# Mixer gates: all side projections first, the last four gate pairs by seven block products

## The chip, the cores and the metric

One core of one Trainium2 chip runs the whole program in one launch. The time is device microseconds of one execution; the number given for a kernel is the median of its runs.

## The reference

Three layers follow each other on 512 rows (528 with 16 meta rows in the first two) of width 1024: a layer with differential attention, one with latent attention, and a block that mixes a convolution and a sliding-window attention. Each ends in a gated feed-forward with a convolution of width 3. All is fp32. The change lies in the mixer of the last block:

```
u = rmsnorm(x, norm_mix_w)
proj = u @ w_in + b_in
cb, cc, cx, q, k, v, g_conv, g_attn = split(proj)
y_conv = (cb * causal_dwconv(cc * cx, conv_mix_w)) @ w_conv_out
y_attn = sliding_window_attention(rope(q), rope(k), v, sinks) @ w_attn_out + b_attn_out
merged = sigmoid(g_conv) * y_conv + sigmoid(g_attn) * y_attn
x = x + merged @ w_mix_out
```

## The kernel before

Activations are held transposed: 128 channels on the partitions, the 512 rows along the free dimension, eight such tiles for the width of 1024. Each fp32 operand is held as two fp32r parts, hi and lo, and a product is three matmuls per 128 channels of contraction: hi hi, hi lo, lo hi (`lin`, L331 to 345).

Weights come through `Weights`. A plan lists the chunks in the order of use; `get` hands out the next chunk and, with it, splits the two that follow and loads the three that follow. A load goes by SP's queue into one of three `raw` buffers. A split is a cast on ACT to `whi` (L176) and a subtraction to `wlo`, on DVE in two halves of 512 columns (L184), or, for one chunk in four, on POOL in pieces of 256 columns (L114).

The feed-forwards compute some of their products in another way, which the change brings to the gates. Two weight tiles (a and b of one f) against two halves of the rows and two halves of the contraction make a two by two block product; `Seven` gets it with seven block products of 12 matmuls each instead of eight, and adds the results together in PSUM and with u1 and u2. Its inputs T are differences of the activations, made once per feed-forward. Its weights are of four kinds: "a" is a chunk as loaded (with its partner in a second buffer, `rawA`), and "s", "t", "d" come from four sums that POOL makes of the two loads (`combine`: 512 columns each, in halves of 256, L114). "s" and "d" have a single buffer each.

The mixer (L1651) first makes Y, the convolution's result, and OT, the attention's, both as hi and lo. Then, in the stage around the change, it goes over eight tiles t. For each it computes two gates (`pg`, 24 matmuls each, X against a chunk of `w_in2`), multiplies them by the norm R on DVE (L1821), takes the sigmoid on ACT (L1822); then the two sides, `pyc` from Y (24 matmuls) and `pya` from OT (12), which DVE takes out of PSUM while it multiplies by the gates (L1826, L1829). POOL adds the two (L1830, below called the join) and the sum is split to MG on ACT and DVE (L450, L451). After that `proj_h` multiplies MG by `w_mo` (`po`) and adds into h.

A scheduler sets the order of the instructions on every engine when the program is built; where code runs inside `in_order`, PE keeps the order in which it is written. Each engine then runs its instructions in that order, and a waiting instruction holds all behind it on its engine.

Of the kernel before, what the change touches and what calls it, by code (L numbers as in the profile page):

```python
# [21 lines left out]
P = 128  # L22
D = 1024
KD = D // P
META = 16
SEQ = 512
NT = META + SEQ
# [15 lines left out]
def _layout_params():  # L43
# [38 lines left out]
class Weights:  # L82
# [126 lines left out]
class Pair:  # L209
# [5 lines left out]
    def at(self, k, s, e):  # L215
        c = slice(s - self.t0, e - self.t0)
        return self.hi[:, k, c], self.lo[:, k, c]


class Net:  # L220
    def __init__(self, ctx, tc, ins, out):
        self.tc, self.nc, self.I, self.out = tc, tc.nc, ins, out
# [1383 lines left out]
    def tables2(self):  # L1606
# [40 lines left out]
            nc.vector.tensor_copy(bandb, band)  # L1647
        self.tables = C, S, bandb


    def mixer(self):  # L1651
        nc, tc = self.nc, self.tc
        scale = 64 ** -0.5
        with ExitStack() as cx:
            e = cx.enter_context
            X, xcx = self.X, self.xcx
            xp = e(tc.tile_pool(name="m2x", bufs=1, side="right", reuse_waits="tile"))
            tp = xcx.enter_context(tc.tile_pool(name="m2t", bufs=2, reuse_waits="tile"))
            acx = ExitStack()
            psm = acx.enter_context(tc.tile_pool(name="m2pm", bufs=2, space=PSUM, reuse_waits="tile"))  # L1660
            pss = acx.enter_context(tc.tile_pool(name="m2ps", bufs=1, space=PSUM, reuse_waits="tile"))
# [3 lines left out]
            R = self.norm2(pss, "s")[:, META:]  # L1665
# [7 lines left out]
            Y = self.xpair(xp, "Y2", KD, META)  # L1673
# [27 lines left out]
            C, S, bandb = self.tables  # L1701
            at = acx.enter_context(tc.tile_pool(name="m2at", bufs=2, reuse_waits="tile"))
# [38 lines left out]
            t = pst.tile([P, 512], F32, tag="t", name=self.n("vt"))  # L1741
# [5 lines left out]
            OT = self.xpair(xp, "OT2", 4, META)  # L1747
# [62 lines left out]
            MG = self.xpair(e(tc.tile_pool(name="m2g", bufs=1, side="right", reuse_waits="tile")), "MG", KD, META)  # L1810
            for t in range(8):
                wgc = [(self.W.get(("w_in2", 30 + t, 0)), 0)]
                wga = [(self.W.get(("w_in2", 38 + t, 0)), 0)]
                wco = [(self.W.get(("w_co", t, 0)), 0)]
                wao = [(self.W.get(("w_ao", t, 0)), 0)]
                g = []
                for w, b, tag in ((wgc, 30 + t, "y"), (wga, 38 + t, "pr")):
                    ps = psm.tile([P, 512], F32, tag="mm", name=self.n("pg"))
                    self.lin(ps, w, X, META, NT)
                    z = tp.tile([P, SEQ], F32, tag=tag, name=self.n("sg"), bufs=2)  # L1820
                    nc.vector.tensor_tensor(z, ps, R, op=ALU.mult)  # L1821
                    nc.scalar.activation(z, z, AF.Sigmoid, bias=self.pc("b_in", b))  # L1822
                    g.append(z)
                ps = psm.tile([P, 512], F32, tag="mm", name=self.n("pyc"))
                self.lin(ps, wco, Y, META, NT)
                nc.vector.tensor_tensor(g[0], ps, g[0], op=ALU.mult)  # L1826
                ps = psm.tile([P, 512], F32, tag="mm", name=self.n("pya"))
                self.lin(ps, wao, OT, META, NT)
                nc.vector.scalar_tensor_tensor(g[1], ps, self.pc("b_ao", t), g[1], op0=ALU.add, op1=ALU.mult)  # L1829
                nc.gpsimd.tensor_tensor(g[0], g[0], g[1], op=ALU.add)  # L1830
                self.split(*MG.at(t, META, NT), g[0])
            xcx.close()
            self.open_x("ffn2_norm", META)
            self.proj_h(psm, "w_mo", MG, REAL)

# [127 lines left out]
```

## Time and profile before

| | us |
|---|---|
| median of 3 runs | 2060.43 (2058.05 to 2063.83) |
| the profiled execution | 2064.14 |
| its span | 2062.4 |
| PE, DVE, ACT, POOL busy | 2036.0, 1400.2, 980.5, 719.1 |

The profile is of one execution. PE's busy time is modelled, so full busy does not mean full speed; how long a group of matmuls takes is read from the chain of waits. In rows of groups the mean of one instruction is in ns. Records of neighbours on one engine can overlap by some hundredths of a us.

### The profile page before, as it was taken

The page shows a single profiled execution, that of the slowest core. Times are in us where ns is not written, and L with a number is a line of the kernel's source. Part 1 is how long each engine was busy: PE and PEld are TensorE (multiplying, and loading weights), DVE is VectorE, ACT ScalarE, POOL GpSimd, SP SyncE. Part 2 cuts the span into 40 slices and gives each one's busy share as a digit, 9 for nine tenths or more (in the row PEclk, how much of TensorE's full clock was granted, in tenths as well). Part 3 has the DMA queues.
Part 4 walks back from the last instruction along what each step waited for, and adds up shares of the span by engine and source line. Part 5 has one row for each costly group of instructions (what it writes and reads, how often), then busy time and mean ns, then how long its engine had stood idle before and what let it go on. Part 6 is the DMA issues. An engine that isn't in the chain of part 4 may idle for free.

```text
span 2062.4 us, 36284 instructions
## 1 busy us (share of the span) xinstructions
PE 2036.0 (99%) x14314; PEld 1884.8 (91%) x14314; DVE 1400.2 (68%) x2548; ACT 980.5 (48%) x1967; POOL 719.1 (35%) x818
## 2 busy tenths in 40 slices
PE   8999999999999999999999999999999999999998
PEld 8999899999999989899899898888888889999897
DVE  8788768667677576668667687675433358667684
ACT  6666545434355455455435355454332335445353
POOL 5222252435353331132536355321022242436452
PEclk9999999999999999999999999999999999999999
DMA  5121132333323111032332322222223232322322
GB/s 172 53 62 52 42 105 68 106 93 98 99 84 98 53 41 42 32 99 74 100 102 92 110 85 89 87 92 72 67 81 104 97 113 70 105 93 99 116 72 72
DMA packets 56426, 174.91 MB, mean 85 GB/s; under 512 B 6464, under 2 KB 9408, under 8 KB 56256
## 3 DMA queue, kind: packets, MB, share of 16 engines
q1 hardware_dynamic: 55824, 172.34, 26.4%
q8 instruction: 112, 1.84, 0.4%
q14 instruction: 58, 0.48, 0.1%
q10 hardware_dynamic: 432, 0.27, 0.0%
HBM read 170.45 MB, written 2.10 MB: 84 GB/s over the span
## 4 chain that ended last, share of the span: by engine, by line
PE 87%; DVE 8%; ACT 2%; issue 1%; POOL 1%; DMA 0%; ACTq 0%; DVEq 0%; SPq 0%
PE po L343 24%; PE pf L576 18%; PE pf L343 17%; PE pc L343 6%; PE pg L343 4%; PE pyc L343 2%; PE pq L343 2%; PE s L767 2%; DVE wlo L184 2%; PE ph L343 2%; PE pm L343 2%; PE pd L343 1%; PE o L1422 1%; PE pya L343 1%; DVE nm L777 1%
## 5 line engine op out<-in xcount | busy, mean ns | idle before, releaser
L176 ACT CAST whi<-raw 128x512 fp32r<-128x512 f32 (+4 forms) x484 | 384.7, 808 | 532.9 <-PE po L343 154.5
L114 POOL TENSOR_TENSOR wlo<-raw,whi 128x256 fp32r<-128x256 f32 (+1 forms) x316 | 273.9, 894 | 572.7 <-ACT whi L176 537.3
L184 DVE TENSOR_TENSOR wlo<-raw,whi 128x512 fp32r<-128x512 f32 (+2 forms) x590 | 410.7, 731 | 50.6 <-ACT whi L176 47.3
L343 PE MATMUL pf<-Xl,whi 128*128 128x256 f32 (+2 forms) x960 | 271.2, 283 | 0.9 <-DVE Xl L454 0.9
L343 PE MATMUL pf<-Xh,whi 128*128 128x256 f32 (+2 forms) x960 | 271.4, 283 | 0.0
L343 PE MATMUL pf<-Xh,wlo 128*128 128x256 f32 (+2 forms) x960 | 271.4, 283 | 0.0
L343 PE MATMUL po<-Gh,wlo 128*128 128x512 f32 (+2 forms) x710 | 239.4, 338 | 0.0
L343 PE MATMUL po<-Gl,whi 128*128 128x512 f32 (+2 forms) x710 | 238.5, 337 | 0.0
L343 PE MATMUL po<-Gh,whi 128*128 128x512 f32 (+2 forms) x710 | 235.6, 340 | 0.0
L343 PEld LDWEIGHTS pf<-Xl,whi 128*128 128x128 f32 x960 | 181.3, 189 | 1.2 <-DVE Xl L454 1.1
L343 PEld LDWEIGHTS pf<-Xh,whi 128*128 128x128 f32 x960 | 181.6, 189 | 0.0
L343 PEld LDWEIGHTS pf<-Xh,wlo 128*128 128x128 f32 x960 | 181.6, 189 | 0.0
L576 PE MATMUL pf<-Tl,whi 128*128 128x264 f32 (+2 forms) x576 | 162.4, 282 | 0.0
L576 PE MATMUL pf<-Th,whi 128*128 128x264 f32 (+2 forms) x576 | 162.3, 282 | 0.0
L576 PE MATMUL pf<-Th,wlo 128*128 128x264 f32 (+2 forms) x576 | 162.3, 282 | 0.0
L343 PEld LDWEIGHTS po<-Gh,wlo 128*128 128x128 f32 x710 | 133.5, 188 | 16.8
L343 PEld LDWEIGHTS po<-Gl,whi 128*128 128x128 f32 x710 | 133.6, 188 | 15.2
L343 PEld LDWEIGHTS po<-Gh,whi 128*128 128x128 f32 x710 | 132.5, 188 | 14.8
L576 PE MATMUL pf<-Xh,whi 128*128 128x264 f32 (+2 forms) x432 | 121.9, 282 | 0.0
L576 PE MATMUL pf<-Xh,wlo 128*128 128x264 f32 (+2 forms) x432 | 121.9, 282 | 0.0
L576 PE MATMUL pf<-Xl,whi 128*128 128x264 f32 (+2 forms) x432 | 121.9, 282 | 0.0
L585 DVE SCALAR_TENSOR_TENSOR ct<-am,par,ct 128x512 f32<-128x512 f32 (+4 forms) x132 | 114.5, 867 | 5.6 <-ACT ct L581 4.6
(434 smaller groups left out, 5496.3 us busy)
## 6 DMA issues: line engine op xcount, KB each, us to landing
raw<-in_w_in_dram SPq DMA_DIRECT2D x134, 512.0 KB, 3.5
raw<-in_w_up_dram SPq DMA_DIRECT2D x44, 512.0 KB, 3.3
raw<-in_w_qkv_dram SPq DMA_DIRECT2D x24, 512.0 KB, 3.6
raw<-in_w_out_dram SPq DMA_DIRECT2D x32, 384.0 KB, 3.2
raw<-in_w_out_dram SPq DMA_DIRECT2D x32, 320.0 KB, 2.9
raw<-in_w_o_dram SPq DMA_DIRECT2D x16, 512.0 KB, 3.5
raw<-in_w_dn_dram SPq DMA_DIRECT2D x16, 384.0 KB, 3.2
raw<-in_w_dn_dram SPq DMA_DIRECT2D x16, 320.0 KB, 2.9
```

The lines of the kernel that those rows point to most:

```text
L114: self.net.nc.gpsimd.tensor_tensor(d[:, c], a[:, c], b[:, c], op=op)
L176: nc.scalar.copy(h[:, c0 : c0 + z], r)
L184: nc.vector.tensor_tensor(l[:, c], r[:, a:b], h[:, c].bitcast(F32), op=ALU.subtract)
L343: nc.tensor.matmul(ps, w, x, start=first and i == 0, stop=i == len(ops) - 1, skip_group_check=not first)
L576: nc.tensor.matmul(ps[:, :H], a, b, start=first and i == 0, stop=i == len(ops) - 1, skip_group_check=not first)
L585: nc.vector.scalar_tensor_tensor(t[:, z:], am[:, a : a + n - z], w, t[:, z:], op0=ALU.mult, op1=ALU.add)
L767: nc.tensor.matmul(s[:, :w], qa[:, q0 : q0 + P], ka[:, k0:k1], start=z == 0, stop=z == len(ops) - 1 and not masked,)
L777: nc.vector.reduce_max(nm[:, j : j + 1], s[:, :w], axis=AX.X, negate=True)
L1422: nc.tensor.matmul(o[:, i, j, :], st[n, "pt", j][:, b * P : (b + 1) * P], V[:, b, c], start=n % 4 == j == b == 0, stop=False,)
```

## The change

The mixer now computes all eight pairs of sides first, right after the two gates of the first tile, and keeps them in fp32 in the memory that will hold MG's parts (`Row`: one tile per part and row). After that Y and OT are not needed, and their memory takes the T tiles, the second load buffers and the "s", "d" and u tiles. Tiles 1 to 3 have plain gates (`PLAIN = 4`). Tiles 4 to 7 take both gates of a tile in seven block products. The differences T are made of X while the plain pairs run: POOL adds X's hi and lo (L1692), DVE makes four differences of 256 columns per k (L1698 to L1701), ACT and DVE split them. Each unit's first block is put ahead of the last block of the unit before.

```diff
+PLAIN = 4
...
+        pl += [c("w_in2", 30), c("w_in2", 38)]
         for t in range(8):
-            pl += [c("w_in2", 30 + t), c("w_in2", 38 + t), c("w_co", t), c("w_ao", t)]
+            pl += [c("w_co", t), c("w_ao", t)]
+        end = []
+        for t in range(1, 8):
+            if t < PLAIN:
+                pl += [c("w_in2", 30 + t), c("w_in2", 38 + t)]
+                continue
+            aps = c("w_in2", 30 + t)[1] + c("w_in2", 38 + t)[1]
+            u = {z: (("w_in2", 30 + t, z), aps if z == "a" else [], 4 if z == "d" else 8, P, z) for z in "astd"}
+            pl += [u["a"], *end, u["s"], u["t"]]
+            end = [u["d"]]
+        pl += end
...
+    def gates(self, tc, tp, psm, X, R, MG, sides, first, plain):
...
+            gp = cx.enter_context(tc.tile_pool(name="m2w", bufs=2, reuse_waits="tile"))
+            self.W.more = gp
+            T = [gp.tile([P, 4, 4, H], F32R, name=self.n("T" + c), tag="T" + c, bufs=1) for c in "hl"]
+
+            def differences(k):
+                x = [tp.tile([P, SEQ], F32, tag=g, name=self.n("x"), bufs=1) for g in ("cc", "cx")]
+                for j in range(2):
+                    xh, xl = X.at(4 * j + k, META, NT)
+                    nc.gpsimd.tensor_tensor(x[j], xh.bitcast(F32), xl.bitcast(F32), op=ALU.add)
...
+                nc.vector.tensor_tensor(d[0][:, 0], b12, b11, op=ALU.subtract)
+                nc.vector.tensor_tensor(d[1][:, 0], b22, b12, op=ALU.subtract)
+                nc.vector.tensor_tensor(d[0][:, 1], d[1][:, 0], b11, op=ALU.add)
+                nc.vector.tensor_tensor(d[1][:, 1], b21, d[0][:, 1], op=ALU.subtract)
+                for z in range(2):
+                    self.split(*(t[:, 2 * z : 2 * z + 2, k, :] for t in T), d[z])
...
+            def weigh(t, i, z):
+                nc.vector.tensor_tensor(z, z, sides[i][t], op=ALU.mult)
+
+            def gate(t, i, z):
+                nc.vector.tensor_tensor(z, z, R, op=ALU.mult)
+                nc.scalar.activation(z, z, AF.Sigmoid, bias=self.pc("b_in", 30 + 8 * i + t))
+                weigh(t, i, z)
+
+            def join(t, g):
+                nc.gpsimd.tensor_tensor(g[0], g[0], g[1], op=ALU.add)
+                self.split(*MG.at(t, META, NT), g[0])
...
+            for t in range(PLAIN):
+                g = pair() if t else first
+                for i in range(2):
+                    if t:
+                        plain(t, i, g[i])
+                    weigh(t, i, g[i])
+                join(t, g)
+                if t == 0:
+                    for k in range(4):
+                        differences(k)
+
+            def seven(t):
+                g = pair()
+                lo, hi = slice(0, H), slice(H, SEQ)
+                bank = lambda p: p.tile([P, 512], F32, tag="mm", name=self.n("pg"))
+                wa = self.W.get(("w_in2", 30 + t, "a"))
+                A = bank(self.psg)
+                block(A, wa, 0, (0, 0))
+                u1 = gp.tile([P, H], F32, tag="u1", name=self.n("u1"), bufs=1)
+                nc.scalar.copy(u1, A[:, :H])
+                yield
+                ws = self.W.get(("w_in2", 30 + t, "s"))
+                C = bank(psm)
+                block(C, ws, 0, 0)
+                nc.scalar.copy(g[1][:, hi], C[:, :H])
+                yield
+                block(A, ws, 4, 1, False)
+                u2 = gp.tile([P, H], F32, tag="u2", name=self.n("u2"), bufs=1)
+                nc.scalar.copy(u2, A[:, :H])
+                yield
+                B = bank(psm)
+                block(B, wa, 4, (1, 0))
+                nc.vector.tensor_tensor(g[0][:, lo], u1, B[:, :H], op=ALU.add)
+                yield
+                wt = self.W.get(("w_in2", 30 + t, "t"))
+                block(A, wt, 0, 2, False)
+                nc.vector.tensor_tensor(g[1][:, hi], A[:, :H], g[1][:, hi], op=ALU.add)
+                yield
+                block(C, wt, 4, (1, 1), False)
+                nc.vector.tensor_tensor(g[0][:, hi], u2, C[:, :H], op=ALU.add)
+                gate(t, 0, g[0])
+                yield
+                block(A, self.W.get(("w_in2", 30 + t, "d")), 0, 3, False)
+                nc.scalar.copy(g[1][:, lo], A[:, :H])
+                gate(t, 1, g[1])
+                join(t, g)
+                yield
...
@@ mixer
-            for t in range(8):
-                wgc = [(self.W.get(("w_in2", 30 + t, 0)), 0)]
...
+            first = [tp.tile([P, 2 + SEQ], F32, tag="pr", name=self.n("sg"))[:, :SEQ] for _ in range(2)]
+            for i in range(2):
+                gate(0, i, first[i])
             for t in range(8):
...
+                for i, (name, src) in enumerate((("w_co", Y), ("w_ao", OT))):
+                    w = [(self.W.get((name, t, 0)), 0)]
+                    ps = psm.tile([P, 512], F32, tag="mm", name=self.n("py" + "ca"[i]))
+                    self.lin(ps, w, src, META, NT)
+                    sides[i].append(MG.tile(t, i, F32))
+                    if i:
+                        nc.scalar.activation(sides[i][t], ps, AF.Identity, bias=self.pc("b_ao", t))
+                    else:
+                        nc.vector.tensor_copy(sides[i][t], ps)
+            ycx.close()
+            self.gates(tc, tp, psm, X, R, MG, sides, first, gate)
             xcx.close()
```

Two places in the built order. The first is POOL's queue. Before, in the gate stage, it alternates between the pieces of one weight split in four chunks and the join of one tile:

```order
L114 TENSOR_TENSOR wlo_17981<-raw_0_17978,whi_17980 128x256 x4
L1830 TENSOR_TENSOR sg_18014<-sg_18014,sg_18042 128x512
L114 TENSOR_TENSOR wlo_18109<-raw_0_18106,whi_18108 128x256 x4
L1830 TENSOR_TENSOR sg_18142<-sg_18142,sg_18170 128x512
L114 TENSOR_TENSOR wlo_18237<-raw_0_18234,whi_18236 128x256 x4
L1830 TENSOR_TENSOR sg_18270<-sg_18270,sg_18298 128x512
```

Now, from the second plain pair's weights on (x is a sum for the differences, rawS, raw_0 and raw_1 are the weight sums, the two joins are those of tiles 1 and 2):

```order
L116 TENSOR_TENSOR raw_1_18410<-raw_0_18408,raw_1_18410 128x256 x2
L1692 TENSOR_TENSOR x_18144<-Xh_15571,Xl_15572 128x512
L1729 TENSOR_TENSOR sg_18157<-sg_18157,sg_18158 128x512
L116 TENSOR_TENSOR raw_0_18278<-rawS_18322,raw_0_18278 128x256 x2
L116 TENSOR_TENSOR raw_0_18278<-raw_0_18278 128x256 x2
L1729 TENSOR_TENSOR sg_18236<-sg_18236,sg_18237 128x512
L116 TENSOR_TENSOR rawS_18576<-raw_1_18548 128x256 x2
L116 TENSOR_TENSOR raw_1_18548<-raw_0_18546,raw_1_18548 128x256 x2
L116 TENSOR_TENSOR raw_0_18408<-rawS_18432,raw_0_18408 128x256 x2
L116 TENSOR_TENSOR raw_0_18408<-raw_0_18408 128x256 x2
```

Ahead of these rows stand, since the last side, two rawS and two raw_1 pairs, one `wlo` pair and three more x. The sums of the third unit (rawS_18576, raw_1_18548) stand ahead of the last sums of the second (raw_0_18408), and all of them behind the join of tile 2.

The second is ACT's queue. Before, in the gate stage, casts of weights and sigmoids alternate:

```order
L176 CAST whi_17980<-raw_0_17978 128x1024
L1822 ACTIVATE sg_18042<-sg_18042,par 128x512
L176 CAST whi_18088<-raw_0_17987 128x1024
L176 CAST whi_18095<-raw_0_18093 128x512
L450 CAST MGh_17574<-sg_18014 128x512
L176 CAST whi_18101<-raw_0_18099 128x1024
```

Now, where the first seven-product unit begins (pg_18412 is its bank A, u_1905 its u1, u_1907 its u2, whi_18540 the "t" weights of the second unit, whi_18519 its "s" weights):

```order
L478 CAST mgh_18311<-sg_18236 128x512
L178 CAST whi_18427<-raw_0_18408 128x1024
L1966 ACTIVATE sg_18315<-sg_18315,par 128x512
L178 CAST whi_18540<-raw_1_18410 128x512
L178 CAST whi_18540<-raw_0_18408 128x512
L1966 ACTIVATE sg_18316<-sg_18316,par 128x512
L1756 COPY u_1905_18425<-pg_18412 128x256
L1761 COPY sg_18401<-pg_18441 128x256
L178 CAST whi_18519<-rawS_18432 128x512
L178 CAST whi_18519<-raw_0_18408 128x512
L478 CAST mgh_18394<-sg_18315 128x512
L1765 COPY u_1907_18467<-pg_18412 128x256
```

The copy of u1 stands behind a cast of raw_0_18408, the last weight sum of the second unit, and behind the sigmoid of tile 3's second gate; the copy of u2 stands behind two casts of the second unit's "s" weights and the cast of tile 3's MG.

## Rows read from the trace of the kernel before

**Rows 1.** The page's part 1, whole span: engine, busy us (share), instructions.

```profile
PE 2036.0 (99%) x14314; PEld 1884.8 (91%) x14314; DVE 1400.2 (68%) x2548; ACT 980.5 (48%) x1967; POOL 719.1 (35%) x818
```

**Rows 2.** Chain of waits, gate stage: start us, us, engine, tile, line, instructions.

```profile
1490.31 11.86 PE pg L343 x48
...
1510.58 11.00 PE pg L343 x48
1521.58 5.60 PE pyc L343 x24
1527.17 2.80 PE pya L343 x12
```

**Rows 3.** Chain of waits, last feed-forward.

```profile
1695.93 10.12 PE pf L343 x72
...
1738.29 2.83 PE pf L343 x24
...
1790.32 9.89 PE pf L576 x84
```

**Rows 4.** Stretches: us; PE, PEld, DVE, ACT, POOL busy (instructions); granted clock; DMA.

```profile
1490.00:1646.00 156.00, 156.00 (x674) 126.83 (x673) 52.28 (x78) 45.85 (x56) 34.33 (x39) 0.99 0.28 90
1860.00:1920.00 60.00, 60.00 (x512) 60.00 (x511) 47.89 (x74) 31.04 (x55) 35.96 (x37) 1.00 0.29 96
1483.00:1490.30 7.30, 5.06 (x38) 4.45 (x37) 3.33 (x5) 2.29 (x4) 0.00 (x0) 0.88 0.22 72
1694.60:1700.00 5.40, 5.36 (x33) 5.36 (x34) 1.32 (x2) 1.17 (x2) 5.33 (x8) 0.71 0.31 119
```

**Rows 5.** Groups by form, 1490 to 1691: busy us, mean ns | idle before.

```profile
L1830 POOL TENSOR_TENSOR sg<-sg,sg 128x512 f32<-128x512 f32 x8 | 13.0, 1623 | 43.3 <-DVE sg L1829 43.3
L1822 ACT ACTIVATE sg<-sg,par 128x512 f32<-128x512 f32 x16 | 11.5, 719 | 0.0
L1821 DVE TENSOR_TENSOR sg<-pg,R 128x512 f32<-128x512 f32 x16 | 11.1, 692 | 42.6 <-PE pg L343 42.6
```

**Rows 6.** Groups by form, feed-forward, 1740 to 1980.

```profile
L184 DVE TENSOR_TENSOR wlo<-raw,whi 128x512 fp32r<-128x512 f32 x67 | 51.9, 807 | 6.4 <-ACT whi L176 6.0
L114 POOL TENSOR_TENSOR wlo<-raw,whi 128x256 fp32r<-128x256 f32 x36 | 36.1, 1026 | 74.0 <-ACT whi L176 74.0
L176 ACT CAST whi<-raw 128x512 fp32r<-128x512 f32 x37 | 22.2, 619 | 23.2 <-PE pf L343 7.1 <-POOL raw L114 6.9 <-PE pf L576 3.6
L114 POOL TENSOR_TENSOR raw<-raw 128x256 f32<-128x256 f32 x20 | 19.3, 976 | 0.0
L114 POOL TENSOR_TENSOR rawS<-raw 128x256 f32<-128x256 f32 x16 | 14.6, 932 | 22.2 <-DMA raw<-in_w_up_dram 22.2
L184 DVE TENSOR_TENSOR wlo<-rawS,whi 128x512 fp32r<-128x512 f32 x9 | 8.3, 925 | 7.0 <-ACT whi L176 7.0
L666 ACT COPY u<-pf 128x256 f32<-128x256 f32 x9 | 3.3, 365 | 1.7 <-PE pf L576 1.7
```

**Rows 7.** Groups by form, DVE, 1490 to 2050: the feed-forward's differences.

```profile
L556 DVE TENSOR_TENSOR d<-d,x 128x256 f32<-128x256 f32 x4 | 2.6, 657 | 0.0
L552 DVE TENSOR_TENSOR d<-x 128x256 f32<-128x256 f32 x4 | 1.8, 447 | 0.0
```

**Rows 8.** Instructions in order of time, POOL: start us, us, instructions at the end.

```profile
1647.20 1.29 POOL L1830 TENSOR_TENSOR sg<-sg,sg 128x512 f32<-128x512 f32 x1 [5.40 <-DVE sg L1829]
...
1785.27 1.45 POOL L114 TENSOR_TENSOR raw<-raw 128x256 f32<-128x256 f32 x2
...
1798.94 2.33 POOL L114 TENSOR_TENSOR wlo<-raw,whi 128x256 fp32r<-128x256 f32 x2
```

**Rows 9.** Instructions in order of time, DVE.

```profile
1799.44 1.22 DVE L184 TENSOR_TENSOR wlo<-rawS,whi 128x512 fp32r<-128x512 f32 x1
...
1804.09 0.68 DVE L184 TENSOR_TENSOR wlo<-raw,whi 128x512 fp32r<-128x512 f32 x1
```

**Rows 10.** The page's part 6: queue, count, KB each, us to landing.

```profile
raw<-in_w_up_dram SPq DMA_DIRECT2D x44, 512.0 KB, 3.3
```

More of the change, by code (lines that the diff above doesn't have):

```diff
@@ L217, in at, with __init__, tile @@
         return self.hi[:, k, c], self.lo[:, k, c]
+class Row:
+    def __init__(self, pool, t0):
+        self.pool, self.t0, self.tiles = pool, t0, {}
+    def tile(self, k, i, dtype):
+        return self.pool.tile([P, NT - self.t0], dtype, tag=f"{'hl'[i]}{k}", name=f"mg{'hl'[i]}{k}{dtype == F32R:d}")
+    def at(self, k, s, e):
+        if k not in self.tiles:
+            self.tiles[k] = [self.tile(k, i, F32R) for i in range(2)]
+        return [t[:, s - self.t0 : e - self.t0] for t in self.tiles[k]]
 class Net:
@@ L1648, in tables2, with block, pair @@
         self.tables = C, S, bandb
+    def gates(self, tc, tp, psm, X, R, MG, sides, first, plain):
+        nc = self.nc
+        H = SEQ // 2
+        with ExitStack() as cx:
+            gp = cx.enter_context(tc.tile_pool(name="m2w", bufs=2, reuse_waits="tile"))
[6 more added lines that the diff above has]
+                    nc.gpsimd.tensor_tensor(x[j], xh.bitcast(F32), xl.bitcast(F32), op=ALU.add)
+                (b11, b12), (b21, b22) = [(t[:, :H], t[:, H:]) for t in x]
+                d = [
+                    tp.tile([P, SEQ], F32, tag=g, name=self.n("d"), bufs=z).rearrange("p (t c) -> p t c", t=2)
+                    for g, z in (("cb", 1), ("y", 2))
+                ]
+                nc.vector.tensor_tensor(d[0][:, 0], b12, b11, op=ALU.subtract)
[4 more added lines that the diff above has]
+                    self.split(*(t[:, 2 * z : 2 * z + 2, k, :] for t in T), d[z])
+            def block(ps, w, c, x, first=True):
+                ops = []
+                for k in range(4):
+                    if isinstance(x, int):
+                        xh, xl = (t[:, x, k, :] for t in T)
+                    else:
+                        xh, xl = X.at(4 * x[0] + k, META + x[1] * H, META + x[1] * H + H)
+                    hi, lo = w[0][:, c + k, :], w[1][:, c + k, :]
+                    ops += [(hi, xh), (hi, xl), (lo, xh)]
+                for i, (a, b) in enumerate(ops):
+                    nc.tensor.matmul(
+                        ps[:, :H], a, b, start=first and i == 0, stop=i == len(ops) - 1, skip_group_check=not first
+                    )
+            def weigh(t, i, z):
[7 more added lines that the diff above has]
+                self.split(*MG.at(t, META, NT), g[0])
+            def pair():
+                g = [p.tile([P, 2 + SEQ], F32, tag=tag, name=self.n("sg")) for p, tag in ((tp, "pr"), (gp, "g"))]
+                return [t[:, :SEQ] for t in g]
+            for t in range(PLAIN):
[6 more added lines that the diff above has]
+                if t == 0:
+                    for k in range(4):
+                        differences(k)
[35 more added lines that the diff above has]
+                yield
+            with self.in_order():
+                last = iter(())
+                for t in range(PLAIN, KD):
+                    u = seven(t)
+                    next(u)
+                    next(last, None)
+                    for _ in range(5):
+                        next(u)
+                    last = u
+                next(last, None)
@@ L1656, in mixer @@
             X, xcx = self.X, self.xcx
-            xp = e(tc.tile_pool(name="m2x", bufs=1, side="right", reuse_waits="tile"))
             tp = xcx.enter_context(tc.tile_pool(name="m2t", bufs=2, reuse_waits="tile"))
+            ycx = ExitStack()
+            xp = ycx.enter_context(tc.tile_pool(name="m2x", bufs=1, reuse_waits="tile"))
             acx = ExitStack()
@@ L1809, in mixer @@
             psm = e(tc.tile_pool(name="m2pz", bufs=6, space=PSUM, reuse_waits="tile"))
-            MG = self.xpair(e(tc.tile_pool(name="m2g", bufs=1, side="right", reuse_waits="tile")), "MG", KD, META)
-            for t in range(8):
-                wgc = [(self.W.get(("w_in2", 30 + t, 0)), 0)]
[L1813 to L1831, printed above, removed]
@@ new lines, in mixer, with gate @@
+            MG = Row(e(tc.tile_pool(name="m2g", bufs=1, side="right", reuse_waits="tile")), META)
+            sides = [[], []]
+            def gate(t, i, z):
+                w = [(self.W.get(("w_in2", 30 + 8 * i + t, 0)), 0)]
+                ps = psm.tile([P, 512], F32, tag="mm", name=self.n("pg"))
+                self.lin(ps, w, X, META, NT)
+                nc.vector.tensor_tensor(z, ps, R, op=ALU.mult)
+                nc.scalar.activation(z, z, AF.Sigmoid, bias=self.pc("b_in", 30 + 8 * i + t))
```

1 line of the change is left out of this document (added).

## The prediction

> **What bounds the kernel now.** I read the page's busy times first [rows 1]: PE is busy 99% of the span, DVE 68%, POOL 35%. What PE issues is the time, unless the change makes it wait. The chain of waits [rows 2] shows the stage that is changed: eight times 48 gate matmuls, 24 of the convolution side and 12 of the attention side, with no other engine between them. One gate pair takes 11.00 us once the clock is up, a side row 5.60 + 2.80 = 8.40 us. The chain of the last feed-forward [rows 3] shows the blocks that the change brings into the gates: 84 matmuls of 256 columns in a row take 9.89 us, 118 ns each against 11.00/48 = 229 ns for 512 columns. The stretches [rows 4] show how much room the other engines have: in the gates DVE is busy 52.3 of 156 us and POOL 34.3; in a feed-forward stretch with two seven-product units per plain one, 47.9 and 36.0 of 60.
>
> **The change, part by part.** The sum is made against the profiled execution's own time, 2064.1 us (span 2062.4), which lies 3.7 us above the median 2060.4 of the runs; I carry the difference over to the median.
>
> *Blocks.* A plain pair is 48 matmuls, 11.00 us [rows 2]; seven blocks of 12 are 84 matmuls, 9.89 us [rows 3]. Four pairs: 4 x 1.11 = 4.4 us less on PE. That is all the change can give.
>
> *Moved sides.* The eight side rows keep their 8.40 us each and only stand together. What they add, a copy on DVE (0.69) and an activation on ACT (0.72) per row [rows 5], lies beside 8.40 us of PE, and DVE is busy a third of this stage [rows 4]; cost 0. Uncovered it would be 1.4 per row. The eight multiplications by the side, now apart from eviction, are counted in DVE's queue below.
>
> *Where the sevens begin.* On the time axis of before, first gates and sides end at 1490.3 + 11.9 + 8 x 8.40 = 1569.4, the three plain pairs at 1602.4. The first seven-product unit's third block adds into the bank of its first, so it must find that bank copied to u1 by ACT: due at 1602.4 + 2 x 1.41 = 1605.2. In the feed-forward a plain piece of 2.83 us stands between these two blocks; here only one block of 1.41 does. In the new order of ACT the u1 copy stands behind a cast that needs the last of POOL's weight sums for the *second* unit, and behind the sigmoid of the last plain gate. So POOL's and DVE's queues decide.
>
> POOL: nothing of the new weights can start before the last side block, whose operands' memory the second load buffer takes over; 3.3 us for the load [rows 10] gives 1572.7. From there POOL has, in order, 14 half-width operations and 5 wide additions up to the second plain pair's join, the join, then 8 half-width sums up to the one that ACT waits for. A half takes 0.93 to 0.98, a split half 1.03 [rows 6], a wide one 1.62 [rows 5].
>
> DVE: from 1570.1 (first cast of the differences) up to the product that this join needs: 23 operations of 512 columns on SBUF, 4 out of PSUM at 0.69 [rows 5], 11 of 256 columns. Their price depends on POOL. With POOL silent a split takes 0.68 [rows 9] and a small operation 0.45 [rows 7]; beside POOL's sums 0.93 [rows 6] and 0.66 [rows 7]; on the average of a feed-forward stretch 0.81 [rows 6], and 0.55 for the small ones as the middle of their two rows.
>
> - Silent: 23 x 0.68 + 2.8 + 11 x 0.45 = 23.4, product at 1593.5. POOL comes to the join at 1572.7 + 12 x 0.95 + 2 x 1.03 + 5 x 1.62 = 1594.3, ends it at 1595.9, eight sums end at 1603.5, cast 0.62, sigmoid 0.72, copy 0.37 [rows 5, 6]: 1605.2. Stall 0.
> - Average: 27.5, product at 1597.6, join 1599.2. The load for the third unit needs a buffer that a split two operations before the product frees, 1596.0 + 3.3 = 1599.3. Eight sums 7.6, then 1.7: 1608.6. Stall 3.4.
> - Beside POOL: 31.3, product at 1601.4, load 1602.8, sums to 1610.4, copy at 1612.1. Stall 6.9.
>
> POOL has no gap in this stretch and DVE works 27 to 31 of 32 us, so the truth lies between the last two: I take 5.2 us, ends 0 and 14.2 (the second rival).
>
> *Inside the sevens.* The weight buffer of the "s" products is single: after the third block ACT makes two casts of 0.62 and a third of 0.62 for MG before it copies u2 (0.37) [rows 6], 2.2 against the 1.41 of the one block that PE has meanwhile: 0.8, less some overlap of records 0.5; in the next two units, without the third cast, 1.6 against 1.41, 0.2 each. Together 0.9 (0 to 1.2). POOL per unit: 8 x 0.95 + 2 x 1.03 + 1.62 = 11.3 us, PE 9.9. It falls 1.4 us back per unit, and in ACT's order a cast of the fourth unit's sums stands before the third unit's copies: 2.0 us (0, if the first stall has let POOL catch up, to 3.6).
>
> *Clock.* Where PE idles 2.2 of 7.3 us at the end of the attention, the granted clock is 0.88, and the next 48 gate matmuls take 11.86 instead of 11.00 [rows 2, 4]; after the feed-forward's opening wait it is 0.71, and 72 matmuls take 10.12 instead of 3 x 2.83 = 8.49 [rows 3, 4]. A PE that waits some us pays 0.9 to 1.6 more: I take 1.2 once (0 to 3.2).
>
> *End.* After the last block: copy, two multiplications, sigmoid, join, cast and split, 0.4 + 0.7 + 0.7 + 0.7 + 1.6 + 0.6 + 0.7 = 5.4 us; PE has meanwhile some 40 matmuls of the next projection's first outputs, without the last row, 9.2 us. Cost 0; if POOL is over 3.8 us late here, that much.
>
> Sum: -4.4 + 5.2 + 0.9 + 2.0 + 1.2 = **+4.9 us**: 2069.0 against 2064.1, on the median 2065.3.
>
> **Rivals.**
> *The cover holds.* DVE and POOL disturb each other little, the u1 copy is in time, and only the short copies cost (0.9 at most): -3.5 to -4.4, about 2056.5. For it: the feed-forwards run the same sums with PE unbroken for long stretches [rows 3]. Against it: there a plain unit stands between, and DVE has 12 of 60 us free [rows 4].
> *DVE and POOL take turns.* In the feed-forward a POOL half alone takes 0.72, beside DVE 1.16 [rows 8]; a DVE split alone 0.68, beside POOL 1.22 [rows 9], each nearly the sum of both. If they take turns all through the transition, both queues stand in line: DVE 23.4 plus POOL's 14 x 0.72 + 5 x 1.3 [rows 8], less 2.8 in which DVE reads PSUM, 37.2: product at 1607.3. Join 1.3, sums 5.8 with five DVE splits between them (3.4), then 1.7: 1619.5, a stall of 14.2. With 0.9, 2.0 and 1.6 of clock, less 4.4: +14.3, 2074.7, slower. It decides from the point where a DVE split takes over 1.1 us on the average of the transition.
> The Trainium skill, page "SBUF — State Buffer", section "Who interferes with whom", says that VectorE and GpSimd share a port pair under an exclusive lock, for DVE operations with two SBUF inputs too. By that rule nearly every operation of this stretch would stand in line; the pair of rows agrees, the mean of the feed-forward does not, since there they meet only part of the time.
> *The blocks don't come cheaper.* If 84 blocks fed by differences took 48 x 229 ns, nothing would be gained; [rows 3] shows exactly such blocks at 118 ns, so 0.03.
>
> **How the numbers follow.** Forecast 0.50, its own range 2061.5 to 2068.5 (losses 5.5 to 12.5); cover holds 0.28; taking turns 0.17; the rest something else. A measurement of this kernel can tell about 0.3%, 6.2 us, from no change. Faster by more than that: the blocks give only 4.4, so a shift elsewhere must help, 0.06. Slower by more (above 2066.6): the upper part of the forecast, 0.15, and taking turns, 0.17: 0.32. Within: 0.62. The range for eight in ten leaves out the lowest part of the first rival and the upper part of the second: 2056.5 to 2072.0.
>
> **What would show it.** Right: in the new chain of waits 11.00 us three times for the plain pairs, then blocks of 1.41 us with one break of several us at the first unit's third block, ended by ACT's u1 copy, a smaller one at the third unit's fifth block ended by u2, and a granted clock below 0.9 behind the first; POOL without a gap in the 30 us before, its halves at 0.9 or more, DVE above 80% busy. Wrong: blocks without a break (then the cover held), a break that the load or the T tiles end, or sides that take over 8.4 us a row.

## The result, and the profile after

The changed kernel takes 2078.35 us (median of 4 runs, 2074.64 to 2079.85), the kernel before 2062.13 us beside it: a ratio of 1.0076, 95% interval 1.0063 to 1.0089. The profiled executions stand 14.0 us apart (spans 2076.4 and 2062.4 us), and it is these 14.0 us that are accounted for here. The direction of the point forecast was right, its size was not: 2065.3 was forecast (+4.9), and the range ended at 2072.0.

The page's busy times first, against [rows 1]:

```profile
PE 2031.5 (98%) x14458; PEld 1888.1 (91%) x14458; DVE 1453.0 (70%) x2608; ACT 1001.8 (48%) x2015; POOL 767.1 (37%) x850
```

TensorE is busy 4.5 us less, and yet the span is longer: it waits. That the 4.5 lie so near the blocks' -4.4 is chance. From the first gates to the next stage's first product TensorE is busy 202.0 us against 203.4, only 1.4 less, because matmuls at a low clock are in it (below); most of the rest lies ahead of this stage. The waits of TensorE from the first gates to the last of them (line, releaser: us in total, times, longest):

```profile
PE pg L1715 <- ACT u L1756: 11.7, 1, 11.7
PE pg L1715 <- ACT u L1765: 2.3, 2, 1.5
PE pg L1715 <- DVE sg L1773: 1.5, 2, 1.2
```

One wait of 11.7 us, for the copy u1 (L1756) in the first seven-product unit, and 3.8 us in the units behind it. Before, there is no wait in this stage. The stretches (us; PE, PEld, DVE, ACT, POOL busy; granted clock; DMA) show where it builds up, beside [rows 4]:

```profile
1570.00:1604.00 34.00, 34.00 (x159) 28.21 (x158) 32.49 (x37) 14.59 (x23) 26.31 (x23) 1.00 0.27 92
1604.00:1656.00 52.00, 36.54 (x284) 35.52 (x283) 40.18 (x52) 25.62 (x48) 35.55 (x34) 0.87 0.25 81
```

While TensorE runs the three plain pairs, VectorE is busy 32.5 of 34 us. The chain of waits from there on (start us, us, engine, tile, line, instructions):

```profile
1490.62 11.79 PE pg L371 x48
1502.41 5.57 PE pyc L371 x24
...
1604.66 0.61 DVE sg L1720
...
1605.34 1.28 POOL sg L1729
...
1610.79 4.42 POOL raw L116 x5
1615.23 0.62 ACT whi L178
1615.85 0.62 ACT sg L1966
1616.47 0.27 ACT u L1756
1616.78 5.41 PE pg L1715 x24
```

Read from the end: u1 stands behind a sigmoid, that behind a cast of the second unit's weights, that behind GpSimd's sums, these behind the join, and the join behind VectorE's multiplication, which ended at 1605.3. The two blocks after the wait take 5.41 us in place of 2.83 [rows 3]: the clock. The same columns in stretches of 2 us behind the wait, where the number ahead of the last two is the granted clock:

```profile
1619.00:1621.00 2.00, 2.00 (x11) 2.00 (x10) 0.76 (x2) 1.41 (x3) 0.00 (x0) 0.50 0.00 0
...
1623.00:1625.00 2.00, 2.00 (x20) 2.00 (x19) 1.81 (x4) 0.17 (x2) 1.05 (x1) 1.00 0.64 217
```

0.50 is 1.2 GHz, 1.00 is 2.4 GHz; the two blocks cost 5.41 - 2.83 = 2.6 us more. The account from the first gates on: 0.3 us later start (1490.62 against 1490.31 [rows 2]), +11.7 and +3.8 of waits, +2.6 of clock, -4.4 of blocks: 14.0, the difference of the spans. The stage itself ends 14.3 us later (1708.96 against 1694.64), and what follows it is 0.3 us shorter, so the account holds to some tenths of a us.

### The profile page after: what moved, and what is told of

Its sections match the earlier page's. It is cut to its first block, busy times and chain, and to the rows that moved or that the text cites. A ratio compares the mean times of both kernels' runs of the same rounds, so it can differ in the third digit from the quotient of the medians.

```text
span 2076.4 us, 36730 instructions
## 1 busy us (share of the span) xinstructions
PE 2031.5 (98%) x14458; PEld 1888.1 (91%) x14458; DVE 1453.0 (70%) x2608; ACT 1001.8 (48%) x2015; POOL 767.1 (37%) x850
## 4 chain that ended last, share of the span: by engine, by line
PE 84%; DVE 10%; ACT 3%; issue 2%; POOL 1%; DMA 0%; ACTq 0%; DVEq 0%; POOLq 0%; SPq 0%
PE po L371 24%; PE pf L604 17%; PE pf L371 17%; PE pc L371 6%; PE pq L371 2%; DVE wlo L186 2%; PE pyc L371 2%; PE s L795 2%; PE pm L371 2%; PE pd L371 1%; PE ph L371 1%; PE o L1450 1%; PE pya L371 1%; DVE nm L805 1%; ACT whi L178 1%
## 5 line engine op out<-in xcount | busy, mean ns | idle before, releaser
L178 ACT CAST whi<-raw 128x512 fp32r<-128x512 f32 (+4 forms) x496 | 390.1, 800 | 506.7 <-PE po L371 143.8
L186 DVE TENSOR_TENSOR wlo<-raw,whi 128x512 fp32r<-128x512 f32 (+2 forms) x602 | 428.6, 746 | 58.5 <-ACT whi L178 56.2
L116 POOL TENSOR_TENSOR rawS<-raw 128x256 f32<-128x256 f32 x80 | 76.5, 977 | 126.4 <-DMA raw<-in_w_in_dram 86.8
```

The costliest lines, as they stand in the source:

```text
L116: self.net.nc.gpsimd.tensor_tensor(d[:, c], a[:, c], b[:, c], op=op)
L178: nc.scalar.copy(h[:, c0 : c0 + z], r)
L186: nc.vector.tensor_tensor(l[:, c], r[:, a:b], h[:, c].bitcast(F32), op=ALU.subtract)
```

## The experiments

Theory 1: VectorE and GpSimd take turns in the transition (the three plain pairs ahead of the first unit, from 1570 us on), and the in-order queues of GpSimd, ScalarE and u hand that on to TensorE. Theory 2: ScalarE's order alone makes the wait (u1 behind the casts of the second unit's weights). Theory 3: the moved sides themselves cost. A fourth came out of experiments 1 to 8: ScalarE's order and the crowd together, the crowd being the dense work of VectorE and GpSimd in the transition.

Fifteen kernels were run. Medians are given with the ratio to the kernel before on the same chip and its 95% interval; the ratio is the one on record, and not the quotient of the two medians. "First wait" is TensorE's wait for u1 in the first unit.

**1. The sides first, without the units.**

```diff
-PLAIN = 4
+PLAIN = 8
```

> The sides of all four units still stand first, but all eight pairs of gates are computed plainly: no differences and no seven-product units. Theory 1 (VectorE and GpSimd take turns in the transition, and GpSimd's, ScalarE's and u's in-order queues pass it to TensorE): all of the loss lies in the transition and the seven-product units, so this kernel is within 2 us of the one before, 2060 to 2064. Theory 3 (the earlier sides themselves and the room they take cost): 3 us or more above the one before, 2065 or higher.

2062.89 us against 2061.39, ratio 1.0003 (0.9994 to 1.0012). No wait in the gates; they run in one piece:

```profile
1570.51 76.92 PE pg L371 x336
...
1695.74 0.51 PE pf L371 x2
```

The moved sides cost nothing that can be measured; theory 3, which had 3 us or more, falls. Everything lies in the transition and the units.

**2. The differences left out.**

```diff
-nc.gpsimd.tensor_tensor(x[j], xh.bitcast(F32), xl.bitcast(F32), op=ALU.add)
...
-    self.split(*(t[:, 2 * z : 2 * z + 2, k, :] for t in T), d[z])
+    nc.scalar.copy(T[i][:, 2 * j : 2 * j + 2, k, :], z.bitcast(F32).rearrange("p (t c) -> p t c", t=2))
```

> Left out: the differences of the mixer's input. X's own blocks are copied by ScalarE into their place (16 copies), so that VectorE's subtractions and splits and GpSimd's additions of the differences go, while GpSimd's weight sums and all products stay. Theory 1: TensorE's first wait in the seven-product units falls from 11.7 us to under 2 us, all waits there to under 5 us, and the time comes to 2057 to 2061, 2 to 5 us under the one before. Theory 2 (GpSimd's weight sums and ScalarE's order alone hold u back): 5 us or more of the first wait stay, and the time is 2066 or more.

2065.95 us, ratio 1.0019 (1.0011 to 1.0028): 12 us under the changed kernel, but 5 us above what was expected, and as a time at the bound of theory 2 (2066). The waits tell the two apart:

```profile
PE pg L1704 <- ACT u L1745: 2.1, 1, 2.1
PE pg L1704 <- ACT u L1754: 1.9, 2, 1.5
PE pg L1704 <- DVE sg L1762: 1.4, 2, 1.2
```

The first wait falls from 11.7 to 2.1 us, where theory 2 had 5 or more left. All waits are 5.4 us, which uses up the saving of 4.4, so the expected time was too low for its own waits; and it left out the clock: behind a wait of only 2.1 us four blocks take 7.42 in place of 5.66 us.

```profile
1607.16 7.42 PE pg L1704 x48
```

**3. Three of GpSimd's four weight sums left out.**

```diff
+        if self.plan[self.ns][0][0] == "w_in2":
+            return
         self.sums(a[1][:, lo], a[0][:, lo], a[1][:, lo], ALU.subtract)
```

> Left out: three of the four sums of weight rows that GpSimd makes for each seven-product unit; the differences stay. Theory 1: GpSimd comes to the unit's other rows sooner and the first wait of 11.7 us falls to 2 to 7 us; the time is 2066 to 2073. Rival (VectorE's work on the differences alone sets it, GpSimd's sums do not matter): the wait stays above 9 us, and the time at 2075 or more.

2064.83 us, ratio 1.0008 (1.0000 to 1.0017). The first wait is 3.5 us, as theory 1 has it, and the rival falls; the time is 1 us under theory 1's range.

```profile
PE pg L1717 <- ACT u L1758: 3.5, 1, 3.5
```

Experiments 2 and 3 together: without the differences (VectorE's work on them and GpSimd's additions) 2.1 us of the wait are left, without three of the four weight sums 3.5, with both 11.7. With either left out the rest is nearly in time; together they are far later. Two pieces of work that only stand in line, with some slack ahead of them, would do the same; whether the engines also hold each other up is what experiment 5 asks.

**4. ScalarE in the order of the text.**

```diff
-            with self.in_order():
+            with self.in_order({mybir.EngineType.PE, mybir.EngineType.Activation}):
```

> ScalarE runs the seven-product units in the order of the program text too, so u's first copy stands behind the two sigmoids and no longer behind the casts of the second unit's weights. Theory 2 (ScalarE's order alone makes the wait): the first wait falls from 11.7 us to 4 us or less and the time to about 2070. Theory 1 (the work on GpSimd and VectorE is late whatever the order, so the wait moves to later blocks and later weights): 10 us or more of waits stay in the seven-product units, and the time is 2074 or more.

2086.17 us, ratio 1.0113 (1.0099 to 1.0126), the slowest of all. The first wait falls to 5.5 us, but the wait moves on, to u2 and to the weights:

```profile
PE pg L1715 <- ACT u L1765: 11.3, 3, 4.8
PE pg L1715 <- ACT u L1756: 5.5, 1, 5.5
PE pg L1715 <- DVE wlo L186: 2.5, 3, 1.4
```

Theory 2 falls in this form. In the text's order u2 stands behind the last sigmoid of the unit before and the cast of its sum, for which ScalarE sits idle 2.8 to 3.3 us (VectorE's multiplication) and 2.1 us (GpSimd's join).

**5. GpSimd as busy, but not reading.**

```diff
+        if self.plan[self.ns][0][0] == "w_in2":
+            for z in (a[1][:, lo], a[0][:, lo], a[0][:, hi]):
+                for c in range(0, 512, 256):
+                    for _ in range(4):
+                        self.net.nc.gpsimd.memset(z[:, c : c + 256], 0.0)
+            return
         self.sums(a[1][:, lo], a[0][:, lo], a[1][:, lo], ALU.subtract)
```

> Left out: three of GpSimd's four sums of weight rows for each seven-product unit; in the place of each 256-column sum GpSimd sets the same columns to zero four times over, which costs it about 4 x 0.3 us (estimate from its 1024-column set of 0.96 us and its 128-column set of 0.21 us in the trace of before) against the sum's 0.97 to 1.16 us in the kernel after. So GpSimd is kept as busy but reads nothing. Theory 1 (VectorE and GpSimd take turns when both read two operands in SBUF): VectorE's operations in the transition come nearer to their price alone (T's low halves from 1.06 us to 0.8 or less) and the first wait falls from 11.7 us to 2 to 7 us, time 2064 to 2072. Rival (the length of GpSimd's own queue sets it): the wait stays at 9 us or more, time 2074 or more.

2067.61 us, ratio 1.0030 (1.0020 to 1.0039); the first wait is 6.9 us. Both lie in theory 1's ranges. GpSimd is busy 26.6 us from 1570 to 1604, against 26.3 in the changed kernel. How VectorE fares beside it is seen in the instructions in order of time; first the changed kernel, GpSimd and then VectorE (start us, us, operation, tiles; x2 are two in one row):

```profile
1577.30 2.39 POOL L116 TENSOR_TENSOR wlo<-raw,whi 128x256 fp32r<-128x256 f32 x2
...
1596.52 1.95 POOL L116 TENSOR_TENSOR raw<-rawS,raw 128x256 f32<-128x256 f32 x2 [1.95 <-DVE wlo L186]
1598.43 2.34 POOL L116 TENSOR_TENSOR raw<-raw 128x256 f32<-128x256 f32 x2
...
1577.81 0.68 DVE L1965 TENSOR_TENSOR sg<-pg,R 128x512 f32<-128x512 f32 x1
...
1597.80 1.22 DVE L1720 TENSOR_TENSOR sg<-sg,mgh 128x512 f32<-128x512 f32 x1
1598.94 1.22 DVE L479 TENSOR_TENSOR mgl<-sg,mgh 128x512 fp32r<-128x512 f32 x1
```

and with the sets:

```profile
1596.56 4.40 POOL L145 MEMSET raw<- 128x256 f32 x17 [1.91 <-DVE wlo L192]
...
1597.63 0.68 DVE L1726 TENSOR_TENSOR sg<-sg,mgh 128x512 f32<-128x512 f32 x1
...
1598.84 0.68 DVE L485 TENSOR_TENSOR mgl<-sg,mgh 128x512 fp32r<-128x512 f32 x1
1599.44 0.68 DVE L1971 TENSOR_TENSOR sg<-pg,R 128x512 f32<-128x512 f32 x1
```

The same multiplication by the side and the same split take 1.22 us beside a GpSimd sum and 0.68 beside GpSimd's sets; an operation that reads one of its operands from PSUM (`sg<-pg,R`) takes 0.68 beside either. So it is the reading of two operands in SBUF that makes them wait for each other, not GpSimd's being busy. The Trainium skill, page "SBUF — State Buffer", section "Who interferes with whom", says that a VectorE instruction with two SBUF inputs contends with a GpSimd instruction that reads SBUF, and not with one that only writes it; this run agrees in both halves. T's low halves came down to 0.92 us only, not to 0.8, since the other GpSimd work (splits and additions for the differences) still reads. Of the 8.2 us that experiment 3 took away (11.7 to 3.5), 4.8 go with the reading alone (11.7 to 6.9); the other 3.4 go with the length of GpSimd's queue, which the sets keep, and behind which ScalarE's cast ahead of u1 waits.

**6. The differences early.** They are made in place during the sides, in empty rooms; only the split into T stays where it was.

```diff
+rooms = [(tp, "cc"), (tp, "cx"), (tp, "y"), (tp, "y"), (tp, "cb"), (self.nrm, "sq"), (self.const, "C2"), (self.const, "S2")]
...
+nc.vector.tensor_tensor(b22, b22, b12, op=ALU.subtract)
...
-nc.vector.tensor_tensor(d[1][:, 0], b22, b12, op=ALU.subtract)
```

> Nothing is left out: the additions and subtractions of all four groups of differences are made during the sides (VectorE and GpSimd are idle for two thirds of it), in place, in rooms that stand empty then; only the split into T stays in the transition. Theory 1: as with the differences left out, the first wait falls to 1 to 4 us, all waits in the units are 4 to 7 us, and the low clock behind the wait costs 2 us less than in the kernel after; time 2063 to 2067. Rival (the first wait comes from the weights' path alone, or the moved work hurts the sides): 7 us or more of the first wait stay, or waits appear in the sides; time 2070 or more.

2075.49 us, ratio 1.0070 (1.0058 to 1.0083).

```profile
PE pg L1702 <- ACT u L1743: 5.4, 1, 5.4
PE o L1916 <- ACT ptS L1913: 3.5, 2, 1.8
PE ot L1933 <- DVE os L1929: 3.0, 1, 3.0
```

The first wait falls by 6.3 us, to 5.4, less than expected, though under the rival's 7. The time is the rival's (2070 or more), and the rival was right that the moved work hurts, though not in the sides: it crept into the end of the attention ahead of them, where TensorE now waits 3.5 and 3.0 us (1.5 and 0.8 before).

**7. Six plain pairs, two units.**

```diff
-PLAIN = 4
+PLAIN = 6
```

> Six pairs of gates plain, the last two by seven products: about 19 us more for the transition, half the saving (2.2 us by the forecast's own count). Theory 1: no first wait, 1 to 3 us of waits in the second unit; time 2060 to 2063. Rival (whatever the time before it, the first unit waits for its own weights' chain of sums): a first wait of 4 us or more, time 2065 or more.

2067.84 us, ratio 1.0033 (1.0021 to 1.0046). The rival's numbers came (4 us or more, 2065 or more): with 22 us more, 4.5 us of the first wait are still there. Its reason, the first unit's own sums, did not. The chain ahead of it:

```profile
1628.27 3.06 POOL raw L116 x3
...
1631.36 0.62 ACT whi L178
1631.97 0.62 ACT sg L1966
1632.60 0.27 ACT u L1756
```

These are the sums of the *second* unit, for which ScalarE's cast waits ahead of u1. More time before the first unit does not make them early: GpSimd sat idle for 2.7 us ahead of them, until VectorE had split the second unit's own load. This was theory 4: a part of the wait of 11.7 us is ScalarE's order after all, and the crowd is the rest.

**8. Early differences, two units apart** (sixth and eighth pair, a plain pair between them).

```diff
-PLAIN = 4
+KINDS = "PPPPPSPS"
...
```

> Early differences as in the other kernel of this call, and two seven-product units, the sixth and the eighth pair, with a plain pair between them, so that GpSimd has two pairs' time for one unit's sums. Theory 1 (the units wait only because GpSimd's and VectorE's work comes too thick): no wait over 0.5 us in the gates, the clock stays up, and the saving of 2.2 us is kept: 1.5 to 3 us under the kernel before, 2058.5 to 2060. Rival (the saving is lost elsewhere): the same as before or slower.

2065.88 us, ratio 1.0021 (1.0012 to 1.0030). No wait at all in the gates, as expected, but the time is the rival's; it is lost where experiment 6 lost it, at the end of the attention (again 3.5 and 3.0 us), and the first gates start at 1494.99.

**9. u1 and u2 ahead of the next unit's casts,** on ScalarE alone, the rest of its order left free.

```diff
+with tc.issue_after(u2_at[-1].ins) if u2_at else ExitStack():
+    wa = self.W.get(("w_in2", 30 + t, "a"))
...
-nc.scalar.copy(u2, A[:, :H])
+u2_at.append(nc.scalar.copy(u2, A[:, :H]))
...
+with tc.issue_after(u2_at[-1].ins):
+    wd = self.W.get(("w_in2", 30 + t, "d"))
```

> Nothing left out; on ScalarE alone, the casts of a unit's weights that wait for GpSimd's sums are put behind the unit before's second copy u2, instead of ahead of its first copy u1 (in the kernel after they stand ahead of it). Theory 4 (of the 11.7 us of the first wait about 4.5 come from these casts ahead of u1, as the wait with six plain pairs shows, the other 7 from the crowded transition): the first wait is 4 to 7 us, all waits 5 to 9 us, time 2064 to 2070. Rival (the crowd alone): first wait 9 us or more, time 2073 or more.

2072.06 us, ratio 1.0052 (1.0038 to 1.0066). The first wait is 8.0 us: 3.7 us went with the order, less than the 4.5 of theory 4. Wait and time lie between theory 4's ranges and the rival's, so neither is met. The rest, as the chain now ends, is VectorE's line up to the sigmoid of the last plain gate (its multiplication by the norm, L1970, ends it), behind which u1 still stands:

```profile
1612.45 0.61 DVE sg L1970
...
1613.09 0.72 ACT sg L1971
1613.81 0.27 ACT u L1759
```

**10. The same order with six plain pairs.** Experiments 7 and 9 in one.

```diff
-PLAIN = 4
+PLAIN = 6
...
```

> The same order on ScalarE with six plain pairs and two units. Theory 4: the first wait of 4.5 us, which more time before the units did not remove, is gone (under 0.5 us), and so is the low clock behind it; 5 to 7 us under the kernel with six plain pairs, 2060 to 2062.5. Rival (the wait of 4.5 us is GpSimd's and VectorE's lateness and not the queue): 2 us or more of it stay, time 2064 or more.

2065.56 us, ratio 1.0014 (1.0005 to 1.0022). The wait falls from 4.5 to 1.9 us, not to nothing: the last plain gate's sigmoid again. The time is in the rival's range (2064 or more), the wait just under its 2 us. Nine blocks behind the wait take 14.38 us in place of 9 x 1.415 = 12.74: 1.6 us of clock.

```profile
1630.24 14.38 PE pg L1715 x108
```

**11. Two units apart, differences as in the changed kernel.** As experiment 8, without its early differences.

> Two units, the sixth and the eighth pair, with a plain pair between, and ScalarE's order left to itself: no second unit's sums are due near the first unit's copies. Differences as in the kernel after. Theory 4: no wait over 0.5 us in the gates; time 2059 to 2062, the same as or up to 2 us under the kernel before. Rival: a wait of 2 us or more stays; 2064 or more.

2066.69 us, ratio 1.0022 (1.0013 to 1.0031). Against the expectation, and as the rival had it, a wait of 3.5 us stays, at the sigmoid of the last plain gate, whose multiplication out of PSUM stands in VectorE's line. With the differences early (experiment 8) it was gone: the crowd.

**12. Three units** (fifth, seventh and eighth pair), copies ahead of the casts.

```diff
-PLAIN = 4
+KINDS = "PPPPSPSS"
...
```

> Three units, the fifth, seventh and eighth pair, with ScalarE's copies ahead of the casts as above. Saving 3.3 us (three quarters of the forecast's 4.4). Theory 4: the first unit comes at the same time as in the kernel after and pays the transition's crowd alone: first wait 2 to 5 us, and about 2 us of low clock behind it; time 2061 to 2065. Rival (no wait, saving kept): 2057 to 2059.

2070.71 us, ratio 1.0043 (1.0031 to 1.0055). The first wait is 7.1 us, near experiment 9's 8.0 and more than the 2 to 5 expected, and the time is 6 us above the expected range; a second wait of 1.9 us has come at the seventh pair, where the chain runs over GpSimd, which has the plain pair's splits besides the units' sums. Behind this second wait the clock stays at 1.00, and nine blocks take 12.86 us:

```profile
1637.64 12.86 PE pg L1716 x108
```

**13. Both edits, the attention left alone.** Copies ahead of the casts, and early differences that VectorE starts behind the attention's last product, GpSimd's third and fourth group behind its second.

```diff
+with tc.issue_after(os_at[-1].ins):
+    nc.vector.tensor_tensor(b22, b22, b12, op=ALU.subtract)
...
```

> All four units; ScalarE's copies ahead of the second unit's casts, and all differences made early, VectorE's part behind the attention's last product and GpSimd's third and fourth group behind its second, so that the attention is not disturbed. Theory 4 (the wait is the sum of the casts ahead of u1 and of the crowd): first wait 1 to 4 us, all waits in the units 2 to 6 us, time 2061 to 2066. Rival (the weights' sums alone, two readers on SBUF, hold the units back): first wait 5 us or more, time 2067 or more.

2068.42 us, ratio 1.0029 (1.0019 to 1.0040); the profiled span is 2065.9 us, 3.5 above the one of before.

```profile
PE pg L1702 <- DVE sg L1763: 2.5, 2, 2.2
PE pg L1702 <- ACT u L1755: 1.9, 2, 1.3
PE pg L1702 <- ACT u L1746: 1.5, 1, 1.5
```

The first wait is 1.5 us: with order and crowd both changed, 10.2 of the 11.7 us are gone. 4.4 us in the later units are left; the stretch from 1604 to 1656 us has VectorE busy 43.4 and GpSimd 35.5 of its 52 us, so that four units in a row leave these two few gaps, and a granted clock of 1.00:

```profile
1604.00:1656.00 52.00, 46.08 (x359) 43.85 (x359) 43.44 (x57) 26.93 (x49) 35.53 (x33) 1.00 0.24 79
```

The waits came as theory 4 had them, the time did not: it is above the 2066 expected, in the rival's range. The attention is nearly left alone; TensorE waits 2.4 us for ScalarE there (1.5 before).

**14. The same with two units apart.** `KINDS = "PPPPPSPS"`.

> The same edits with two units, the sixth and the eighth pair, a plain pair between. Theory 4: no wait over 0.5 us in the gates, no low clock, saving 2.2 us less about 1 us at the mixer's start that every kernel with the sides first has: 2059.5 to 2061.5, 0 to 2 us under the kernel before. Rival (two units save nothing): 2062.5 or more.

2062.12 us against 2062.04, ratio 0.9999 (0.9989 to 1.0008). No wait in the gates, no low clock; the time lies between the 2061.5 expected and the rival's 2062.5. From the first plain gate to the next stage's first product, 1570.83 to 1693.75, it takes 122.9 us; experiment 1 takes 125.2 (1570.51 to 1695.74):

```profile
1570.83 43.96 PE pg L372 x192
...
1693.75 0.51 PE pf L372 x2
```

2.3 us less, for two units the saving that was forecast (2.2). The first gates start 1.3 us later than before (1491.66), so that nothing measurable is left of it in the whole.

**15. The same with three units.** `KINDS = "PPPPSPSS"`.

> The same edits with three units, the fifth, seventh and eighth pair. Theory 4: first wait 0 to 3 us; without a wait 2058.5 to 2060, with one of 2 us and the low clock behind it 2061 to 2063. Rival: waits of 5 us or more, 2065 or more.

2068.01 us, ratio 1.0024 (1.0015 to 1.0033). The first unit waits 0.5 us; the second waits 3.9, where GpSimd's sums are late as in experiment 12, and pays the clock behind it; the time is 5 us above the expected range, in the rival's.

No version that was run beats the kernel before; experiments 1 and 14 cannot be told from it.

## Why the forecast was wrong, step by step

*Blocks, -4.4:* right. At full clock nine blocks take 12.86 us (experiment 12), 1.43 each against the 1.41 counted, and two units saved 2.3 us in experiment 14.

*Moved sides, 0:* right. A row of 5.57 + 2.79 us against 5.60 + 2.80 [rows 2], and experiment 1.

*Where the units begin, and who is waited for:* right. The third block was due at about 1605, and u1, behind a cast of the second unit's weights and a sigmoid, released it.

*The size of that wait, 5.2 us:* this is the step that failed, by the price of VectorE's operations in the transition; the wait measured 11.7. The forecast read VectorE's price in the transition from the feed-forward, where the two engines meet part of the time, and chose between the average there (0.81) and beside GpSimd's sums (0.93 [rows 6], itself a mean of nine that did not all meet). Its count of 38 operations up to the product is exact; their prices are not. The groups by form from 1570 to 1606 show what was paid:

```profile
L479 DVE TENSOR_TENSOR Tl<-d,Th 128x512 fp32r<-128x512 f32 x8 | 8.4, 1055 | 2.7 <-ACT Th L478 2.7
L186 DVE TENSOR_TENSOR wlo<-raw,whi 128x512 fp32r<-128x512 f32 x9 | 8.1, 923 | 0.0
L1698 DVE TENSOR_TENSOR d<-x 128x256 f32<-128x256 f32 x3 | 4.0, 1331 | 0.0
```

16.5 us for 17 splits, 0.97 each. The eleven small operations that were counted at 0.55 to 0.66 took 0.97 on the average (10.7 us in all), those of L1698 1.33. The product that the join needs ended at 1605.3; the forecast's two cases had 1597.6 and 1601.4. That GpSimd had no gap here, from which the forecast took its middle, was wrong too: GpSimd was busy 26.3 of 34 us and idle 4.6 us for this product.

```profile
1605.34 1.27 POOL L1729 TENSOR_TENSOR sg<-sg,sg 128x512 f32<-128x512 f32 x1 [4.57 <-DVE sg L1720]
```

The load of the third unit's rows, which needs a buffer that VectorE frees, was there at 1607.7 (1599.3 and 1602.8). From there on the working held: eight sums in 7.5 us (7.6), then 1.5 us on ScalarE (1.7). Even its slower case gave 6.9 us, and taking the middle of two cases, both priced too low, made it 5.2.

*The rivals:* "taking turns" had the mechanism that the forecast priced too low, as experiment 5 shows, but not all through: a split took 0.97 on the average, not over 1.1, and GpSimd had gaps. That its +14.3 us meets the difference of the profiles (14.0) is luck: its wait was too long (14.2), its clock (1.6 for 2.6) and its waits in the units (2.9 for 3.8) too short. It had 0.17 of the chance. "The cover holds" had 0.28 and was far off.

*Inside the units, 0.9 + 2.0:* 3.8 us, near in sum. The waits for u2 came (2.3 us, the longest 1.5 at the third unit's fifth block, as foretold); the other 1.5 us, for VectorE's addition out of the bank that the last block needs (L1773), were not in the forecast.

*Clock, 1.2:* 2.6. The rows it was read from had shorter waits ahead of them.

*What the forecast did not separate:* its u1 stood behind a cast that no time ahead of the units could make early. Experiment 9 puts 3.7 of the 11.7 us on this order, and experiment 10 takes 2.6 of the 4.5 away that experiment 7 had left; the other 8 us are the crowd.

The medians of experiments 2, 11 and 13 lie some 3 us further above the kernel before than their profiled spans do. That is the executions that were profiled: the one of the kernel before (2064.14) is 1.8 to 2.8 us above the medians beside these experiments, those of the three experiments 0.5 to 1.7 below theirs. And each kernel with the sides first waits 1.5 us for VectorE at 1317 us, ahead of the attention. In the profiles most of that is balanced: the execution profiled before has a stretch from 1294.4 to 1297.4 us at a granted clock of 0.50, where matmuls of 512 columns are 0.43 us apart and not 0.23, some 1.4 us; the changed kernel and experiment 1 have 1.00 there. Left open is whether that holds in the other executions, which no trace shows.

## What to carry to other kernels

Price an operation of VectorE from the stretch in which GpSimd works as densely as it will after the change, and not from an average over a stage in which they seldom meet; where both read two operands in SBUF, the sum of their times is the upper bound of each (alone 0.68 and 0.72 us [rows 8, 9]; where they met, VectorE's took 1.22). A kernel that TensorE bounds at 99% gives a cheaper product back as soon as its feeders come late: count the feeders' work per unit first, and then ask of each copy that releases a block which casts, of *which* unit, stand ahead of it in its engine's queue. Units that are fed apart, with their differences made early, keep their saving (experiment 14) where units in a row lose it (experiment 13).

## What the runs showed of the hardware

- A short wait can cost more than itself. Behind a wait of 1.9 us nine blocks ran 1.6 us long (experiment 10), behind 2.1 us four blocks 1.8 us (experiment 2), behind 11.7 us two blocks 2.6 us (the changed kernel), each with a stretch at a granted clock of 0.50. But behind the second wait of experiment 12 (1.9 us), and in experiment 13 with waits of up to 2.2 us, the clock stayed at 1.00; what tells these cases apart the runs do not show.
- GpSimd sets 256 columns to zero in 0.26 us (17 in 4.40 us), at the same pace beside VectorE's two-operand work, and does not slow it.
